# A three-block model on one core: forget attention in six half-rate stages, and four other waiting products moved

## The chip, the cores and the metric

The kernel runs on one core of a Trainium2 chip. The metric is device time in microseconds (us), the median of several runs. TensorE multiplies (PE in the profile, its weight loads PEld), VectorE (DVE) and ScalarE (ACT) do the elementwise work, GpSimd (POOL) and SyncE (SP) issue transfers here. Results of products land in PSUM, which has eight banks; everything else works in SBUF.

## What is computed

256 tokens of width 1024 go through two blocks of float32 arithmetic. The first has two layers (chunked retention, then MoBA attention), each followed by a squared-relu MLP. The second mixes four branches (a difference attention, a "forgetting" attention, a 31-tap convolution with a layer norm, a short convolution), gates them, adds a cross attention to a memory of 256 rows, and ends in a gated feed-forward. Cut to the parts that the change touches:

```python
# MoBA layer, 8 heads of 128
o = (o_own * a + o_sel * b) / (l_own * a + l_sel * b);  return o @ w_out
h = h + rms_norm(mixer(rms_norm(h, pre)), post);  h = h + rms_norm(sq_relu_mlp(rms_norm(h, mpre)), mpost)

# second block: forgetting attention, 8 heads of 64, c = cumsum(log_sigmoid(f_g + b_fgt))
s = q @ k.T * 64 ** -0.5 + (c_q - c_k);  p = softmax(where(causal, s, -inf));  yf = p @ v
yc = silu(layer_norm(dwconv_causal(...)))
# cross attention, 4 heads of 128
px = softmax(xq @ xk.T * 128 ** -0.5);  x = x + rms_norm((px @ xv) @ w_xo, norm_x_post)
```

## The kernel before, in words

**Weights.** All weights lie in 203 chunks of 128x2048 in the order of use. Each chunk is two pieces of 128x1024; SyncE loads a piece (`raw`), ScalarE copies it to a rounded high part `whi` (line 156), VectorE subtracts to the low part `wlo` (line 162). A product of float32 accuracy is then three products (`mm3`, lines 235 to 237, or `down`, lines 267 to 271): high by high, high by low, low by high.

**Units and ticks.** The program is written as a list of units of TensorE work (24 products of 256 columns, or 12 of 512). After each unit `tick()` is called: it prepares one or two more weight pieces, and lets every active "lane" do one step. A lane is a Python generator, one step up to the next `yield`; so what a lane writes in one step stands on TensorE's queue between two units, and what it needs from ScalarE and VectorE must be ready when TensorE gets there. `pipe(n, (d, f), ...)` makes a lane of `n` items: in step `j` it calls each stage `f` for item `j - d`, the deepest stage first. `slow` holds the convolution taps (line 860): one tap per tick while a lane is active, up to three otherwise. All engines work their queues in the order written; tiles come from pools with a fixed number of buffers (43 big ones of SBUF in `b4`, four PSUM banks in `psw` for short-lived results, four in `psa` for sums), and an instruction that writes a reused buffer waits for its last reader.

**Boundaries.** Between layers, `boundary` runs the last rows of a down projection for tokens 0 to 127 (`down_pass` t = 0), then the same for tokens 128 to 255 (t = 1). While t = 1 runs, VectorE and ScalarE compute the norm of the first half (`chain`); its transposes (`pt`, line 294) are put before the last item of t = 1, or behind it with `late`.

**The places that the change touches.** (1) MoBA's last heads: `moba_pv(6)` and `moba_pv(7)` (line 775) stand among the two halves of item 0 of the output projection, ahead of the boundary (lines 808 to 815). (2) `fgh`, `fgl`, the two parts of the forget gate's weights, are split at lines 910 and 911, behind the convolution's first chunks; `forget_gate` multiplies by them in `ps_ft8` (line 922). (3) The forget lane (lines 1087 to 1140) has four stages for four pairs of heads, a new pair in every step: `forget_s` (scores `sps`, masks on VectorE, exponentials on ScalarE, line 1108), `forget_n` (reciprocal, then four scalings on ScalarE, line 1118), `forget_t` (six transposes to two `ps_ft` banks, two copies on ScalarE, line 1126), `forget_y` (products `ps_fy`, line 1135, split to `brh` and `brl`). In the same steps the difference attention's last part (`ps_dyt`, line 1075) and the short convolution (`sx`, `sy`, lines 1151 to 1163) run. (4) `conv_norm` transposes its normalized values `cxn` at line 884, two yields after it has asked for them. (5) In the cross attention, `xv` (the values, 256x512) is copied from PSUM in one ScalarE instruction per token half, and `cross_o` (line 1337) writes four heads to one bank `ps_xo` and splits it at once to `xoh`, `xol`, on which the output projection `xa` waits.

Of the kernel before, what the change touches and what calls it, by code (L numbers as in the profile page):

```python
# [99 lines left out]
def tile_model(ctx: ExitStack, tc: tile.TileContext, order, wall, x, mem, gains, pparam, rparam, w_fg,  # L100
# [20 lines left out]
    def bank(name):  # L121
        return psw.tile([128, 512], F32, tag="w", name=name)
# [58 lines left out]
    def done(n=1):  # L181

        state["done"] += n
# [32 lines left out]
        while any(g in lanes or g in light or g in slow for g in gs):  # L216
            tick()

    def pipe(n, *stages, wait=0):

        for _ in range(wait):
            yield
        for j in range(n + max(d for d, _ in stages)):
            for d, f in reversed(stages):
                if 0 <= j - d < n:
                    f(j - d)
            yield


# [167 lines left out]
    def down_pass(acc, items, t, first, splits, before_last=None):  # L397
        n = len(items)
        for i in range(n):
            if callable(items[i]):  # L400
                items[i] = items[i]()
            w, ah, al = items[i]
            if i == n - 1 and before_last:
                before_last()
            down(acc, w, ah, al, t, first and i == 0, i == n - 1)
            if i < n - 1:
                if t:
                    done()
                tick(splits[i])

    def boundary(acc, items, first, gpost, gpre, fill0, fill1, mid=None, late=False, splits=((2, 2, 1), (1, 1, 0))):

        gp, gn = gain(gpost), gain(gpre)
        load_sqrt()
        before = state["nraw"], state["nprep"]
        state["nraw"], state["nprep"] = AHEAD

        def x0():
            new_x()
            to_T(xn0, 0, xh2, xl2)

        down_pass(acc, items, 0, first, splits[0])
        xn0 = chain(acc[0], gp, gn, 0, "0", between=mid)
        down_pass(acc, items, 1, first, splits[1], None if late else x0)
        if late:
            x0()
        xn1 = chain(acc[1], gp, gn, 1, "1")  # L430
        done()
        state["nraw"], state["nprep"] = before
        for i, f in enumerate(fill0):
            if i == len(fill0) - 1:
                to_T(xn1, 1, xh2, xl2)
            f()
        for f in fill1:
            f()
# [330 lines left out]
    def moba_pv(hd):  # L769
        i, k = hd // 4, hd % 4  # L770
        if k == 0:
            mo[i] = b4([128, 4, 256], f"moh{i}", F32R), b4([128, 4, 256], f"mol{i}", F32R)
        po = bank("ps_mo")
        for j in range(2):
            nc.tensor.matmul(po[:, 0:256], mv[i][:, j, k * 128:k * 128 + 128],
                             mpT[hd // 2][:, hd % 2, j * 256:j * 256 + 256], start=j == 0, stop=j == 1)
        split(mo[i][0][:, k, :], mo[i][1][:, k, :], po[:, 0:256])
# [28 lines left out]
    moba_pv(4)  # L806
    moba_pv(5)
    it = moba_item(0)
    for t in range(2):
        down(acc, *it, t, True, False)  # L810
        moba_pv(6 + t)
    done()
    items = [moba_item(c) for c in range(1, 4)]
    acts, fill = mlp_start(1)
    boundary(acc, items, False, "ln_mix_post_1", "ln_mlp_pre_1", *fill)
    if upto == 3:
        return finish()
    state["nprep"] = NPREP[3]
# [8 lines left out]
    def nat_spec(name, w, c0):  # L827
        def evac(t, ps):
            if t == 0:
# [2 lines left out]

        return [("cols512", w, c0 // 512, c) for c in range(2)], evac

    boundary(acc, items, False, "ln_mlp_post_1", "norm_mix_pre_2",
             *as_group([nat_spec("av", "w_in_2", A_V), nat_spec("fv", "w_in_2", F_V)]))
    if upto == 4:
# [7 lines left out]
    def br(i):  # L845
        brh[i] = b4([128, 4, 256], f"brh{i}", F32R)
        brl[i] = b4([128, 4, 256], f"brl{i}", F32R)
# [16 lines left out]
    def conv_norm():  # L864
        ba, pts = stat("ba", 4), []
        for t in range(2):
            pts.append(bank("ps_ct"))
            for i in range(4):
                nc.tensor.transpose(pts[t][:, i * 128:i * 128 + 128], yc[:, i, tok(t)], ident)
        yield  # L870
        for t in range(2):
            bs = stat("bs", 6)
            nc.vector.bn_stats(bs, pts[t])
            nc.vector.bn_aggr(ba[:, 2 * t:2 * t + 2], bs)
        r = rstd(ba[:, 1:4:2], 2, 1.0, "ln")
        xns = [t2("cxn") for _ in range(2)]
        for t in range(2):
            nc.vector.tensor_scalar(xns[t], pts[t], ba[:, 2 * t:2 * t + 1], r[:, t:t + 1], op0=ALU.subtract, op1=ALU.mult)
        yield
        yield  # L880
        br(2)
        pts = [bank("ps_ct2") for _ in range(2)]
        for t in range(2):
            transposes(pts[t], xns[t])
        for t in range(2):
            for i in range(4):
                nc.scalar.activation(xns[t][:, tok(i)], pts[t][:, tok(i)], AF.Silu, bias=ppc("ln_b", i), scale=ppc("ln_g", i))
        for t in range(2):
            split(brh[2][:, :, tok(t)], brl[2][:, :, tok(t)], tiles(xns[t]))
        yield  # L890
# [16 lines left out]

    lf = cp.tile([128, 2, 8], F32, name="lf")

    fgh, fgl = [t1(f"fg{i}", (128, 8, 8), F32R) for i in range(2)]  # L910
    split(fgh, fgl, fg)

    cum = t1("cum", (128, 256), F32R)
    head = cp.tile([128, 8], F32R, name="head")
    lf4 = t1("lf4", (128, 2, 128))

    def forget_gate():
        ft = bank("ps_ft8")  # L920
# [36 lines left out]
        nc.vector.scalar_tensor_tensor(ls[:, 2:3], ls[:, 0:1], -1.0, ls[:, 1:2], op0=ALU.mult, op1=ALU.add)  # L957
        nc.vector.tensor_scalar(ls[:, 3:4], ls[:, 2:3], -lambda_init, None, op0=ALU.add)
        nc.vector.tensor_scalar(dn, rp[:, RP_DN:RP_DN + 128], 1.0 - lambda_init, None, op0=ALU.mult)
        nc.vector.memset(lf4, 0.0)  # L960
        nc.vector.tensor_copy(lf4.rearrange("p t (g c) -> p t g c", c=32)[:, :, :, 0:8],
                              lf[:, :, None, :].broadcast_to([128, 2, 4, 8]))
# [6 lines left out]
        pc = bank("ps_cum")  # L969
        nc.tensor.matmul(pc[:, 0:256], lf4[:, 0, :], small[:, C_TRI:C_TRI + 256], start=True, stop=False)  # L970
        nc.tensor.matmul(pc[:, 128:256], lf4[:, 1, :], small[:, C_TRI:C_TRI + 128], start=False, stop=True)
        nc.scalar.activation(cum, pc[:, 0:256], AF.Copy)
        for r in (slice(32, 64), slice(96, 128)):
            nc.vector.tensor_tensor(cum[r, :], pc[r, 0:256], cum[r, :].bitcast(F32), op=ALU.subtract)
# [112 lines left out]
    def forget_s(hp):  # L1087

        st = stat("fst", 16)
        e = b4([128, 2, 384], "fe")  # L1090
        half = [slice(0, 64), slice(64, 128)]
        for t in range(2):
            nk = 128 * (t + 1)
            for c in range(2):
                pick = head[half[c], 2 * hp + c:2 * hp + c + 1].broadcast_to([64, 128])
                nc.tensor.matmul(sps[c][:, KS[t]], pick, cum[half[c], 0:nk], start=True, stop=False)
            for c in range(2):
                nc.tensor.matmul(sps[c][:, KS[t]], fqT[half[c], hp, tok(t)], fkT[half[c], hp, 0:nk], start=False, stop=True)
        for t in range(2):
            msk = small[:, C_MASK + 128 * (1 - t):C_MASK + 256]  # L1100
            for c in range(2):
                nc.vector.tensor_tensor_reduce(e[:, c, KS[t]], sps[c][:, KS[t]], msk, scale=1.0, scalar=NEG,
                                               op0=ALU.add, op1=ALU.max, accum_out=st[:, 2 * t + c:2 * t + c + 1])
        nc.vector.tensor_scalar(st[:, 4:8], st[:, 0:4], -0.125, None, op0=ALU.mult)
        for t in range(2):
            for c in range(2):
                l = 2 * t + c
                nc.scalar.activation(e[:, c, KS[t]], e[:, c, KS[t]], AF.Exp, bias=st[:, 4 + l:5 + l], scale=0.125,
                                     accum_out=st[:, 8 + l:9 + l])
        fp[hp] = e, st  # L1110

    def forget_n(hp):
        e, st = fp[hp]
# [3 lines left out]
                l = 2 * t + c  # L1117
                nc.scalar.activation(e[:, c, KS[t]], e[:, c, KS[t]], AF.Copy, scale=st[:, 12 + l:13 + l])  # L1118

    def forget_t(hp):  # L1120
        e, _ = fp.pop(hp)
        pT = fpT[hp] = b4([128, 2, 384], "fpT")
        for c in range(2):
            pt = bank("ps_ft")
            transposes(pt, e[:, c, :], 3)
            nc.scalar.activation(pT[:, c, :], pt[:, 0:384], AF.Copy)  # L1126

    def forget_y(hp):
        py = bank("ps_fy")
# [7 lines left out]
            br(1)  # L1137
        split(brh[1][:, hp, :], brl[1][:, hp, :], py[:, 0:256])

    fl = lane(pipe(4, (0, forget_s), (1, forget_n), (2, forget_t), (3, forget_y)))  # L1140


    sbt = None
# [182 lines left out]
    for c in range(2):  # L1326
        ws_chunk(("colsat", "w_xq_2", c * 256),
                 lambda ps: nc.scalar.activation(xq[:, 2 * c:2 * c + 2, :], tiles(ps, 256), AF.Copy))
        if c == 0:
            lane(xlane)  # L1330
    as_pair(*nat_spec("xv", "w_xkv_2", 512), mth, mtl)
    drain(xlane)
    xv = nat["xv"]
    oh = b4([128, 4, 256], "xoh", F32R)
    ol = b4([128, 4, 256], "xol", F32R)

    def cross_o(t):
        po = bank("ps_xo")
        for hd in range(4):
            for j in range(2):  # L1340
                nc.tensor.matmul(po[:, hd * 128:hd * 128 + 128], xv[:, j, hd * 128:hd * 128 + 128],
                                 xpT[hd // 2][:, hd % 2, j * 256 + t * 128:j * 256 + t * 128 + 128],
                                 start=j == 0, stop=j == 1)
        split(oh[:, :, tok(t)], ol[:, :, tok(t)], tiles(po))

    cross_o(0)
    acc = [pair("xa0"), pair("xa1")]
# [241 lines left out]
```

## Time and profile before

| | |
|---|---|
| median of 3 runs | 1264.92 us (1264.87 to 1265.36) |
| the profiled execution | 1264.71 us |
| its span in the trace | 1263.0 us |
| granted clock of TensorE over the span | 0.999 |
| busy: PE, PEld, DVE, ACT | 1237.4, 1115.1, 877.7, 678.4 us |
| transfers | 227.43 MB, 180 GB/s |

How to read it: an engine's row in a timeline gives start, duration, source line, the tile written and those read, and in brackets how long the engine had been idle and what ended that. TensorE's products overlap: one of 256 columns is shown with 0.28 us, one of 512 with 0.39, while the next starts after 0.12 or 0.23. So a wait is best read from start to start.

### The profile page before, as it was taken

What the parts mean: (1) busy time and instruction counts of PE and PEld (TensorE: products, weight loads), DVE (VectorE), ACT (ScalarE), POOL (GpSimd) and SP (SyncE); (2) the same over time, 40 slices, a digit from 0 to 9 for tenths busy, and PEclk for the clock granted to TensorE, in tenths of its full rate; (3) what the DMA queues carried; (4) which work ended last, traced back from release to release, by engine and by line L of the source; (5) the groups of instructions that cost most, each with busy time, mean ns of one, the idle gap of its engine ahead of it and who ended that gap; (6) DMA issues with size and microseconds to landing.
All of it is one profiled execution on the core that took longest, in us unless ns stands there. A gap on an engine that the chain in (4) does not pass through costs nothing. (4 is left out here: it accounts for less than half of the span.)

```text
span 1263.0 us, 20014 instructions
## 1 busy us (share of the span) xinstructions
PE 1237.4 (98%) x7870; PEld 1115.1 (88%) x7870; DVE 877.7 (69%) x1537; ACT 678.4 (54%) x1103; POOL 9.3 (1%) x22
## 2 busy tenths in 40 slices
PE   6999999999999999999999999999999999999997
PEld 4888888899988888899998999899999897899996
DVE  6774768755566766765557578688877877588773
ACT  5553445644444765654444545754446575666552
POOL 0000000000000000000000000000000000000000
PEclk9999999999999999999999999999999999999999
DMA  9765564665664535566565644255665564455530
GB/s 342 279 186 156 159 218 166 213 196 178 198 217 134 183 120 180 187 214 190 179 211 181 208 144 141 71 174 170 188 203 197 182 207 163 159 191 185 183 117 34
DMA packets 64206, 227.43 MB, mean 180 GB/s; under 512 B 8048, under 2 KB 8304, under 8 KB 64112
## 3 DMA queue, kind: packets, MB, share of 16 engines
q1 hardware_dynamic: 61808, 217.76, 52.8%
q0 software_dynamic: 2304, 8.39, 2.0%
q8 instruction: 62, 1.02, 0.3%
q14 instruction: 32, 0.26, 0.1%
HBM read 225.08 MB, written 1.05 MB: 179 GB/s over the span
## 5 line engine op out<-in xcount | busy, mean ns | idle before, releaser
L162 DVE TENSOR_TENSOR wlo<-raw,whi 128x1024 fp32r<-128x1024 f32 x406 | 480.1, 1220 | 79.9 <-ACT whi L156 78.8
L156 ACT ACTIVATE whi<-raw 128x1024 fp32r<-128x1024 f32 x406 | 406.8, 1049 | 52.8 <-PE ps_ws L237 14.8
L235 PE MATMUL ps_ws<-xhi,whi 128*128 128x256 f32 x1376 | 391.3, 284 | 1.2 <-ACT fpT L1126 0.9
L236 PE MATMUL ps_ws<-xlo,whi 128*128 128x256 f32 x1376 | 389.3, 283 | 0.0
L237 PE MATMUL ps_ws<-xhi,wlo 128*128 128x256 f32 x1376 | 389.3, 283 | 0.0
L235 PEld LDWEIGHTS ps_ws<-xhi,whi 128*128 128x128 f32 x1376 | 263.8, 192 | 5.9 <-issue 2.5
L236 PEld LDWEIGHTS ps_ws<-xlo,whi 128*128 128x128 f32 x1376 | 263.9, 192 | 1.5
L237 PEld LDWEIGHTS ps_ws<-xhi,wlo 128*128 128x128 f32 x1376 | 263.9, 192 | 0.0
L235 PE MATMUL ps_as<-whi,xhi 128*128 128x512 f32 x352 | 142.2, 404 | 0.3 <-ACT xhi L231 0.3
L236 PE MATMUL ps_as<-wlo,xhi 128*128 128x512 f32 x352 | 137.7, 391 | 0.5 <-DVE wlo L162 0.5
L237 PE MATMUL ps_as<-whi,xlo 128*128 128x512 f32 x352 | 138.1, 392 | 0.0
L268 PE MATMUL mlp<-wlo,act 128*128 128x512 f32 x240 | 93.7, 390 | 0.0
L267 PE MATMUL mlp<-whi,act 128*128 128x512 f32 x240 | 93.5, 390 | 0.0
L237 PEld LDWEIGHTS ps_as<-whi,xlo 128*128 128x128 f32 x352 | 66.2, 188 | 15.3 <-DVE xlo L232 1.1
L236 PEld LDWEIGHTS ps_as<-wlo,xhi 128*128 128x128 f32 x352 | 66.5, 189 | 14.2 <-DVE wlo L162 1.3
L235 PEld LDWEIGHTS ps_as<-whi,xhi 128*128 128x128 f32 x352 | 66.4, 189 | 13.6 <-ACT xhi L231 0.9
L662 DVE SCALAR_TENSOR_TENSOR relu<-ps_ws,relu 128x512 f32<-128x512 f32 x24 | 16.6, 691 | 87.1 <-ACT relu L661 87.1
L661 ACT ACTIVATE relu<-ps_ws 128x512 f32<-128x512 f32 x24 | 14.4, 598 | 113.8 <-PE ps_ws L237 113.8
L271 PE MATMUL mlp<-whi,act 128*128 128x512 f32 x240 | 73.9, 389 | 0.0
L271 PEld LDWEIGHTS mlp<-whi,act 128*128 128x128 f32 x240 | 45.1, 188 | 9.5
L267 PEld LDWEIGHTS mlp<-whi,act 128*128 128x128 f32 x240 | 45.2, 188 | 8.6
L268 PEld LDWEIGHTS mlp<-wlo,act 128*128 128x128 f32 x240 | 45.2, 188 | 8.6
(427 smaller groups left out, 1613.8 us busy)
## 6 DMA issues: line engine op xcount, KB each, us to landing
raw<-in_wall_dram SPq DMA_DIRECT2D x406, 512.0 KB, 4.2
h<-in_x_dram SPq DMA_DIRECT2D x4, 256.0 KB, 5.7
gainln_mix_post<-in_gains_dram POOLq DMA_DIRECT2D x2, 512.0 KB, 5.6
gainln_mlp_pre<-in_gains_dram POOLq DMA_DIRECT2D x2, 512.0 KB, 6.7
gainln_mlp_post<-in_gains_dram POOLq DMA_DIRECT2D x2, 512.0 KB, 7.6
mem<-in_mem_dram POOLq DMA_DIRECT2D x2, 512.0 KB, 5.8
out_dram<-h SPq DMA_DIRECT2D x4, 256.0 KB, 2.9
dec<-in_t_dec_dram SPq DMA_DIRECT2D x2, 384.0 KB, 8.9
```

The lines of the kernel that those rows point to most:

```text
L156: nc.scalar.activation(hi, raw, AF.Copy)
L162: nc.vector.tensor_tensor(lo, raw, hi.bitcast(F32), op=ALU.subtract)
L235: nc.tensor.matmul(o, ah, bh, start=start, stop=False)
L236: nc.tensor.matmul(o, ah, bl, start=False, stop=False)
L237: nc.tensor.matmul(o, al, bh, start=False, stop=stop)
L267: nc.tensor.matmul(acc[t][n], ah[:, k, ts], wh[k][:, ns], start=st, stop=False)
L268: nc.tensor.matmul(acc[t][n], ah[:, k, ts], wl[k][:, ns], start=False, stop=False)
L271: nc.tensor.matmul(acc[t][n], al[:, k, ts], wh[k][:, ns], start=False, stop=False)
L661: nc.scalar.activation(r, ps, AF.Relu)
L662: nc.vector.scalar_tensor_tensor(r, ps, 0.0, r, op0=ALU.max, op1=ALU.mult)
```

## The change

It has five parts. MoBA: both halves of heads 6 and 7 come before the boundary, item 0's second token half moves into the boundary's t = 1 pass as its first item (`ahead`). Forget gate: `fgh`, `fgl` are split before the preceding boundary; `lf4` and `cum` are taken from their pool later. Forget lane: the exponentials become a stage of their own, the transposes of a pair are put in two steps, and a new pair starts in every second step; the lane has 12 steps in place of 7. Convolution norm: one more yield ahead of the transposes of `cxn`. Cross attention: `xv` of the second token half is copied in two halves, and `cross_o` writes two heads to each of two banks, each split by itself.

```diff
-    def pipe(n, *stages, wait=0):
+    def pipe(n, *stages, wait=0, every=1):
-        for j in range(n + max(d for d, _ in stages)):
+        for j in range(every * (n - 1) + 1 + max(d for d, _ in stages)):
             for d, f in reversed(stages):
-                if 0 <= j - d < n:
-                    f(j - d)
+                if 0 <= j - d < n * every and (j - d) % every == 0:
+                    f((j - d) // every)
...
-        down_pass(acc, items, 1, first, splits[1], None if late else x0)
+        down_pass(acc, [*ahead, *items], 1, first or bool(ahead), splits[1], None if late else x0)
...
-    for t in range(2):
-        down(acc, *it, t, True, False)
-        moba_pv(6 + t)
-    done()
+    down(acc, *it, 0, True, False)
+    for hd in (6, 7):
+        moba_pv(hd)
...
-    boundary(acc, items, False, "ln_mix_post_1", "ln_mlp_pre_1", *fill)
+    boundary(acc, items, False, "ln_mix_post_1", "ln_mlp_pre_1", *fill, ahead=[it])
...
+    fgh, fgl = [t1(f"fg{i}", (128, 8, 8), F32R) for i in range(2)]
+    split(fgh, fgl, fg)
     boundary(acc, items, False, "ln_mlp_post_1", "norm_mix_pre_2",
...
         yield
         yield
+        yield
         br(2)
...
-        for t in range(2):
-            for c in range(2):
-                l = 2 * t + c
-                nc.scalar.activation(e[:, c, KS[t]], e[:, c, KS[t]], AF.Exp, ...)
+    def forget_e(hp):
+        e, st = fp[hp]
+        ...
+    def forget_t(hp, c):
+        if c == 0:
+            fpT[hp] = b4([128, 2, 384], "fpT")
+        pt = bank("ps_ft")
+        transposes(pt, fp[hp][0][:, c, :], 3)
+        nc.scalar.activation(fpT[hp][:, c, :], pt[:, 0:384], AF.Copy)
...
-    fl = lane(pipe(4, (0, forget_s), (1, forget_n), (2, forget_t), (3, forget_y)))
+    fl = lane(pipe(4, (0, forget_s), (1, forget_e), (2, forget_n), (3, lambda hp: forget_t(hp, 0)),
+                   (4, lambda hp: forget_t(hp, 1)), (5, forget_y), every=2))
...
+            for sl in (slice(0, 256), slice(256, 512)):
+                nc.scalar.activation(xv[:, t, sl], ps[:, sl], AF.Copy)
...
-        po = bank("ps_xo")
-        for hd in range(4):
+        for i in range(2):
+            po = bank("ps_xo")
+            for k in range(2):
+                hd = 2 * i + k
...
-        split(oh[:, :, tok(t)], ol[:, :, tok(t)], tiles(po))
+            split(oh[:, 2 * i:2 * i + 2, tok(t)], ol[:, 2 * i:2 * i + 2, tok(t)], tiles(po[:, 0:256]))
```

ScalarE's queue in the forget lane, one step of the program before (`fe` are the probabilities, L1118 scales those of one pair, L1108 takes the exponentials of the next, `whi` begins each step):

```order
L156 ACTIVATE whi<-raw 128x1024
L231 ACTIVATE brh_7913<-ps_fy 128x256
L1126 ACTIVATE fpT<-ps_ft 128x384 x2
L1118 ACTIVATE fe<-fe,fst 128x128 x2
L1118 ACTIVATE fe<-fe,fst 128x256 x2
L1108 ACTIVATE fe,fst<-fe,fst 128x128 x2
L1108 ACTIVATE fe,fst<-fe,fst 128x256 x2
L1151 ACTIVATE sx<-ps_ws 128x256
L156 ACTIVATE whi<-raw 128x1024
```

The same place in the changed program, the sixth and seventh step (L1114 now takes the exponentials, L1123 scales, L1130 copies the transposes):

```order
L156 ACTIVATE whi<-raw 128x1024
L231 ACTIVATE brh_7991<-ps_fy 128x256
L1130 ACTIVATE fpT<-ps_ft 128x384
L1114 ACTIVATE fe,fst<-fe,fst 128x128 x2
L1114 ACTIVATE fe,fst<-fe,fst 128x256 x2
L1156 ACTIVATE sx<-ps_ws 128x256
L231 ACTIVATE brh_7661<-ps_dyt 128x4x128
L156 ACTIVATE whi<-raw 128x1024
L1130 ACTIVATE fpT<-ps_ft 128x384
L1123 ACTIVATE fe<-fe,fst 128x128 x2
L1123 ACTIVATE fe<-fe,fst 128x256 x2
```

A step now has either the exponentials of one pair or the scalings of another, and one copy of transposes, where each step had both and two copies.

TensorE's queue at the end of MoBA before: item 0 for t = 0 ends, head 6 follows, then item 0 for t = 1 (`moba_0_4564`).

```order
L271 MATMUL moba_1_4563<-whi,mol_4459 128x512
L775 MATMUL ps_mo<-mpT,mv_4480 128x256 x2
L267 MATMUL moba_0_4564<-whi,moh_4458 128x512
L268 MATMUL moba_0_4564<-wlo,moh_4458 128x512
L267 MATMUL moba_1_4565<-whi,moh_4458 128x512
```

The same place in the changed program:

```order
L271 MATMUL moba_1_4563<-whi,mol_4459 128x512
L777 MATMUL ps_mo<-mpT,mv_4480 128x256 x4
L267 MATMUL moba_0_4562<-whi,moh_4458 128x512
L268 MATMUL moba_0_4562<-wlo,moh_4458 128x512
L267 MATMUL moba_1_4563<-whi,moh_4458 128x512
```

Both heads' products stand together, and t = 0 goes on; the twelve products of item 0 for t = 1 follow behind the whole pass t = 0.

ScalarE's queue at the cross attention before (`xv` values, `xoh` the heads' results):

```order
L831 ACTIVATE xv<-ps_as 128x512
L156 ACTIVATE whi<-raw 128x1024
L231 ACTIVATE xoh<-ps_xo 128x4x128
L395 ACT_TABLE_LOAD
```

and in the changed program:

```order
L1343 ACTIVATE xv<-ps_as 128x256 x2
L156 ACTIVATE whi<-raw 128x1024
L231 ACTIVATE xoh<-ps_xo 128x2x128 x2
L395 ACT_TABLE_LOAD
```

Each of the two copies is now two of half the width; the weight copy stays between them.

## Rows read from the trace of the kernel before

**Rows 1.** The page's first part: busy us, share of span, instructions.
```profile
span 1263.0 us, 20014 instructions
PE 1237.4 (98%) x7870; PEld 1115.1 (88%) x7870; DVE 877.7 (69%) x1537; ACT 678.4 (54%) x1103; POOL 9.3 (1%) x22
```

**Rows 2.** PE's longest wait, whole run: us in total, times, longest.
```profile
PE pt L294 <- DVE xn L391: 10.9, 1, 10.9
```

**Rows 3.** Timeline of PE at MoBA's boundary: start, us, instruction [idle before].
```profile
500.06 0.39 PE L268 MATMUL moba<-wlo,moh 128*128 128x512 f32 x1
500.28 0.61 PE L271 MATMUL moba<-whi,mol 128*128 128x512 f32 x2
501.48 1.09 PE L294 MATMUL pt<-ident,y 128*128 128x128 f32 x8 [0.59 <-DVE y L391]
```

**Rows 4.** Timeline of PE at the forget gate's product.
```profile
736.04 0.28 PE L236 MATMUL ps_ft<-xlo,fg 128*8 128x256 f32 x1
737.28 0.28 PE L237 MATMUL ps_ft<-xhi,fg 128*8 128x256 f32 x1 [0.96 <-DVE fg L232]
737.40 0.28 PE L235 MATMUL ps_ft<-xhi,fg 128*8 128x256 f32 x1
```

**Rows 5.** Timeline of PE in the forget lane, steps 3 to 6 of 7.
```profile
804.04 0.84 PE L294 MATMUL ps_ft<-ident,fe 128*128 128x128 f32 x5 [0.36 <-ACT fe L1118]
...
809.76 0.87 PE L294 MATMUL ps_ft<-ident,fe 128*128 128x128 f32 x6
810.56 0.33 PE L1096 MATMUL sps<-cum,head 64*128 64x128 f32 x2
...
812.61 0.39 PE L235 MATMUL ps_ws<-xhi,whi 128*128 128x256 f32 x1 [0.90 <-ACT fpT L1126]
...
816.48 0.92 PE L294 MATMUL ps_ft<-ident,fe 128*128 128x128 f32 x6
817.99 0.66 PE L294 MATMUL ps_dyt<-ident,dsq 128*128 128x128 f32 x4 [0.58 <-ACT fpT L1126]
...
822.24 0.55 PE L294 MATMUL ps_ft<-ident,fe 128*128 128x128 f32 x3
...
824.18 0.66 PE L294 MATMUL ps_dyt<-ident,dsq 128*128 128x128 f32 x4 [0.32 <-ACT fpT L1126]
825.15 0.39 PE L235 MATMUL ps_ws<-xhi,whi 128*128 128x256 f32 x1 [0.32 <-DVE brl L232]
```

**Rows 6.** Step 4 in the table by windows: length, then busy PE, PEld, DVE, ACT, POOL.
```profile
808.90:815.60 6.70, 5.80 (x52) 4.80 (x50) 3.46 (x14) 6.70 (x24) 0.00 (x0) 1.00 0.28 81
```

**Rows 7.** ACT's groups by line in the forget lane: busy, mean ns | idle before.
```profile
L1118 ACT ACTIVATE fe<-fe,fst 128x128 f32<-128x128 f32 (+1 forms) x16 | 6.0, 445 | 2.9 <-DVE fst L1114 2.9
L231 ACT ACTIVATE brh<-ps_fy 128x256 fp32r<-128x256 f32 x4 | 1.5, 369 | 2.7 <-PE ps_fy L1135 2.7
```

**Rows 8.** Timeline of PE at the convolution norm's transposes.
```profile
954.45 1.28 PE L294 MATMUL ps_ct<-ident,cxn 128*128 128x128 f32 x8 [0.48 <-DVE cxn L878]
```

**Rows 9.** Timeline of ACT at the cross attention.
```profile
1049.31 0.60 ACT L831 ACTIVATE xv<-ps_as 128x512 f32<-128x512 f32 x1 [2.09 <-PE ps_as L237]
1049.80 1.05 ACT L156 ACTIVATE whi<-raw 128x1024 fp32r<-128x1024 f32 x1
1051.88 0.60 ACT L231 ACTIVATE xoh<-ps_xo 128x512 fp32r<-128x512 f32 x1 [1.03 <-PE ps_xo L1341]
```

**Rows 10.** Timeline of PE at the cross attention.
```profile
1049.96 1.83 PE L1341 MATMUL ps_xo<-xpT,xv 128*128 128x128 f32 x14 [0.47 <-ACT xv L831]
1052.53 0.50 PE L267 MATMUL xa<-whi,xoh 128*128 128x512 f32 x1 [0.75 <-ACT xoh L231]
...
1060.76 0.50 PE L267 MATMUL xa<-whi,xoh 128*128 128x512 f32 x1 [0.69 <-ACT xoh L231]
```

**Rows 11.** Timeline of DVE there: the first token half's norm, last step.
```profile
1065.46 0.89 DVE L391 TENSOR_SCALAR y<-y,s 128x512 f32<-128x512 f32 x2
```

**Rows 12.** The page's list of transfers: weight pieces, KB each, us to landing.
```profile
raw<-in_wall_dram SPq DMA_DIRECT2D x406, 512.0 KB, 4.2
```

More of the change, by code (lines that the diff above doesn't have):

```diff
@@ L409, in down_pass, with boundary @@
                 tick(splits[i])
-    def boundary(acc, items, first, gpost, gpre, fill0, fill1, mid=None, late=False, splits=((2, 2, 1), (1, 1, 0))):
+    def boundary(acc, items, first, gpost, gpre, fill0, fill1, mid=None, late=False, splits=((2, 2, 1), (1, 1, 0)),
+                 ahead=()):
         gp, gn = gain(gpost), gain(gpre)
@@ L908, in tile_model @@
     lf = cp.tile([128, 2, 8], F32, name="lf")
-    fgh, fgl = [t1(f"fg{i}", (128, 8, 8), F32R) for i in range(2)]
-    split(fgh, fgl, fg)
-    cum = t1("cum", (128, 256), F32R)
+    fsum = {}
     head = cp.tile([128, 8], F32R, name="head")
-    lf4 = t1("lf4", (128, 2, 128))
     def forget_gate():
@@ L959, in forget_gate @@
         nc.vector.tensor_scalar(dn, rp[:, RP_DN:RP_DN + 128], 1.0 - lambda_init, None, op0=ALU.mult)
+        lf4 = t1("lf4", (128, 2, 128))
         nc.vector.memset(lf4, 0.0)
@@ L971, in forget_gate @@
         nc.tensor.matmul(pc[:, 128:256], lf4[:, 1, :], small[:, C_TRI:C_TRI + 128], start=False, stop=True)
+        cum = fsum["cum"] = t1("cum", (128, 256), F32R)
         nc.scalar.activation(cum, pc[:, 0:256], AF.Copy)
@@ L1095, in forget_s @@
                 pick = head[half[c], 2 * hp + c:2 * hp + c + 1].broadcast_to([64, 128])
-                nc.tensor.matmul(sps[c][:, KS[t]], pick, cum[half[c], 0:nk], start=True, stop=False)
+                nc.tensor.matmul(sps[c][:, KS[t]], pick, fsum["cum"][half[c], 0:nk], start=True, stop=False)
             for c in range(2):
@@ L1104, in forget_s @@
         nc.vector.tensor_scalar(st[:, 4:8], st[:, 0:4], -0.125, None, op0=ALU.mult)
+        fp[hp] = e, st
+    def forget_e(hp):
+        e, st = fp[hp]
         for t in range(2):
@@ L1109, in forget_s @@
                                      accum_out=st[:, 8 + l:9 + l])
-        fp[hp] = e, st
     def forget_n(hp):
@@ L1118, in forget_n @@
                 nc.scalar.activation(e[:, c, KS[t]], e[:, c, KS[t]], AF.Copy, scale=st[:, 12 + l:13 + l])
-    def forget_t(hp):
-        e, _ = fp.pop(hp)
-        pT = fpT[hp] = b4([128, 2, 384], "fpT")
-        for c in range(2):
-            pt = bank("ps_ft")
-            transposes(pt, e[:, c, :], 3)
-            nc.scalar.activation(pT[:, c, :], pt[:, 0:384], AF.Copy)
+    def forget_t(hp, c):
[4 more added lines that the diff above has]
+        nc.scalar.activation(fpT[hp][:, c, :], pt[:, 0:384], AF.Copy)
     def forget_y(hp):
@@ L1330, in tile_model, with xv_evac @@
             lane(xlane)
-    as_pair(*nat_spec("xv", "w_xkv_2", 512), mth, mtl)
+    xv = b4([128, 2, 512], "xv")
+    def xv_evac(t, ps):
+        if t == 0:
+            nc.scalar.activation(xv[:, t, :], ps, AF.Copy)
+        else:
+            for sl in (slice(0, 256), slice(256, 512)):
+                nc.scalar.activation(xv[:, t, sl], ps[:, sl], AF.Copy)
+    as_pair([("cols512", "w_xkv_2", 1, c) for c in range(2)], xv_evac, mth, mtl)
     drain(xlane)
-    xv = nat["xv"]
     oh = b4([128, 4, 256], "xoh", F32R)
@@ L1337, in cross_o @@
     def cross_o(t):
-        po = bank("ps_xo")
-        for hd in range(4):
[L1340 to L1343, printed above, removed]
-        split(oh[:, :, tok(t)], ol[:, :, tok(t)], tiles(po))
+        for i in range(2):
+            po = bank("ps_xo")
+            for k in range(2):
+                hd = 2 * i + k
+                for j in range(2):
+                    nc.tensor.matmul(po[:, tok(k)], xv[:, j, tok(hd)],
+                                     xpT[i][:, k, j * 256 + t * 128:j * 256 + t * 128 + 128], start=j == 0, stop=j == 1)
+            split(oh[:, 2 * i:2 * i + 2, tok(t)], ol[:, 2 * i:2 * i + 2, tok(t)], tiles(po[:, 0:256]))
     cross_o(0)
```

## The prediction

> **What bounds the kernel now.** I read the page's first part first: TensorE is busy 1237.4 of 1263.0 us, the next engine 69% [rows 1]. The end of the program is therefore set by TensorE's queue, and a change that neither adds nor removes products can only move the 25.6 us in which TensorE is idle. Next I read the waits of PE over the whole run: 10.9 us of the idle time is the start of the program, before the first normalized rows exist [rows 2], and no edit comes near it. So all that this change can reach lies in short stalls of 0.3 to 1.2 us in the middle. The view for these is the timeline of PE at each place that the diff names. There the reader is to look at starts, not at the idle time in brackets: a product's shown end is later than the moment at which the next could start, so the bracket is always some 0.15 us short of the true loss (0.96 in brackets, 1.24 against 0.12 from start to start [rows 4]).
>
> **The terms.** The products are the same in number and shape before and after; five stalls are to be priced.
>
> *MoBA's boundary.* The last two products ahead of the transposes start from 500.28 on, the usual spacing is 0.22 to 0.23 (500.06 to 500.28), and the transposes start at 501.48, held by the norm on VectorE [rows 3]: 1.20 - 2 x 0.23 = 0.74 us lost. The change puts twelve products of 0.23, 2.7 us, between the end of t = 0 and these transposes, which is work taken from ahead of the boundary. The norm starts as much earlier as TensorE's sum is ready earlier, so 2.7 us of cover stand against 0.74 of lateness: the stall goes whole, **0.74**. Heads 6 and 7 cost what they cost before; their split is needed only by the third item behind them.
>
> *Forget gate.* The third product waits for the low part `fg` that VectorE writes behind convolution taps: 1.24 from start to start, 0.12 is usual [rows 4]. Splitting it a boundary earlier removes the wait: **1.12**. What it adds is one small instruction each on ScalarE and VectorE ahead of a norm that waits for TensorE anyway; I cost it at nothing. If that cover were gone it would be about 0.4 (two instructions, no more than the 128x256 copy's 0.37 each [rows 7], in part side by side).
>
> *Forget lane.* Waits in the seven steps now: 0.36 in step 3; 0.90 in step 4; in step 5 six transposes and then `ps_dyt` take 1.51 where six undisturbed take 0.80 (809.76 to 810.56), so 0.71; in step 6 six transposes and four `ps_dyt` take 2.91 (822.24 to 825.15) where ten take 1.3 at the pace of 0.80 for six, so 1.6 [rows 5]. Together 3.6. In step 4 ScalarE is busy for all of its 6.70 us [rows 6], and the scalings wait for the reciprocals [rows 7]: the step asks more of ScalarE than TensorE's 24 weight products of 0.12 and the lane's own products cover. Half-rate stages remove this for steps 3 to 5: a step now has four exponentials or four scalings, not both. What stays: the first transposes come one step behind their scalings, whose reciprocal stands on VectorE behind the difference attention's scaling: I take 0.2. And the two `ps_dyt` groups keep their two neighbouring steps, now with one shared PSUM bank (the pool gives the second the first one's bank; before they had two), while the short convolution, the masks and a weight piece stand on VectorE ahead of their last reader. Neither row shows this new order. Its cost is bounded below by 0 and above by a little over today's 1.6 in the step with `ps_dyt`; I take 1.6, the nearest row, since the same readers are late there today. More steps mean more places where the lane's products interrupt the weight products, but each of the eight blocks of half-width products is still entered and left once, so I cost the interruptions at 0 (at most 0.1 for each of the four transposes split in two). Net 3.6 - 1.6 - 0.2, **1.8** (0 to 3.6).
>
> *Convolution norm.* Eight transposes wait 0.48 in brackets and take 1.28 where eight take 1.09 at another place [rows 8, 3], as the second half of their input is late as well: 0.67, with the bracket's shortfall about **0.75**. One more unit of weight products (2.9 us) now stands ahead. What follows, silu and split on ScalarE, ends a step later; the branch products that read it stand several units further on.
>
> *Cross attention.* Token half 0: the second product waits for the whole `xv` copy, which takes 0.60 from 1049.31 [rows 9]; a copy of half the width takes 0.37 [rows 7], so TensorE goes on 0.23 earlier. Then `xa` starts at 1052.53 because `xoh` is made after all sixteen records of `ps_xo` [rows 10]. With two banks the first half of `xoh` needs eight of them. It then hangs on ScalarE: from 1049.31 two copies of 0.37, the weight copy 1.05, and 0.37 for `xoh` give 1051.5, and TensorE's sixteen records end at about 1051.4. Gain 1052.53 - 1051.5 = **1.05**. Token half 1: 0.69 in brackets [rows 10], some 0.85 from start to start, and here ScalarE is free; but then the first half's norm is late next: its last step ends at 1066.35 [rows 11], just as TensorE now starts the transposes. VectorE's split in that chain becomes shorter (its first half lies beside TensorE's second), so I give back 0.1: **0.75**.
>
> [...] The row shows 0.37 for half and 0.60 for the whole [rows 7, 9], so a split costs 0.14. [...]
>
> **The sum.** 0.74 + 1.12 + 1.8 + 0.75 + 1.05 + 0.75 = 6.2 us. The profiled execution took 1264.71, so 1258.5; the median of the three runs is 0.2 above that execution, so I forecast **1258.7**. About 0.2%, 2.5 us, is what a measurement of this kernel can tell from no change: the line is at 1262.4.
>
> **Rivals.**
>
> *A. PSUM banks hold the forget lane, not the pace.* Two of today's waits there are for a bank's reader (`fpT`, `brl` [rows 5]), and the lane now needs a bank in nearly every step, eleven of twelve. For it: the shared bank of `ps_dyt`. Against it: six transposes took two banks in one step, now three take one. If each saved wait returns as a bank wait, the lane gains 0 and the time is 1260.5. The Trainium skill ("Perfetto Trace Analysis", Optimization Strategy) reads gaps that repeat on the saturated engine as a sign that too few PSUM or SBUF buffers are there; the waits for `fpT` in steps 4 to 6 agree with that, the reciprocal wait of the scalings does not. Chance 0.2.
>
> *B. All stalls go.* If the readers of `ps_dyt` keep up once ScalarE has air, 1.8 more are saved, and the brackets' shortfalls another 0.4: 1256.5. Against it: VectorE's queue there is as long as before in the same two steps. Chance 0.15.
>
> *C. Little is left.* Stalls close one after the other on one queue; if TensorE, once earlier, meets the next late input at each place (weight pieces, the norm in [rows 11], silu), only the MoBA and the gate terms stay, 1.86 less 0.4: 1263.2. Against it: no weight piece is waited for at these places in the rows. Chance 0.08.
>
> *D. Slower.* Item 0's four weight buffers are now held until the boundary's second pass, some 11 us longer, and the forget lane's `fe` tiles some twice as long; both share the pool in which pieces land, and loads are issued in order on one queue. A piece takes 4.2 us from issue to landing [rows 12]. If the pieces due behind such a hold come late, TensorE stands for about one landing each: with three of them, 12.6 us, 1271. It decides once the hold exceeds the lead, and eight or nine pieces are prepared ahead at these places in the written order, one of which is used in each unit of 2.9 us. Chance 0.04, and 0.03 of it is over the line.
>
> **How the numbers follow.** The forecast's case has 0.53 (1257.5 to 1259.9, as the lane's residual lies between 0.5 and 2.9), A 0.2, B 0.15, C 0.08, D 0.04. The range takes in B's and A's times with the scatter of their terms, and leaves out C and D and the edges of B, under 0.2: 1256.2 to 1261.4. Faster by over 0.2%: the forecast, A and B, 0.88; within 0.2%: C and a part of D, 0.09; slower: 0.03.
>
> **What would show it.** In the changed profile: no wait of the MoBA transposes for `y`; none of `ps_ft` for `fg`; no wait for `fe` or `fpT` in step 4's place, and the largest wait of the lane at the second `ps_dyt` or the unit behind it; none at `ps_ct`; `xa` starting at the first token half within 0.3 us of the last `ps_xo` record. PE busy stays at about 1237 and the span falls. The prediction is wrong if the lane's waits stay near 3.6 in sum (A), if they vanish (B), or if PE shows new waits for `wlo` or `whi` behind MoBA's boundary or in the forget lane (D).

## The result and the profile after

The changed kernel takes **1258.34 us** (median of 4 runs, 1258.06 to 1259.14) against 1264.89 for the kernel before in the same comparison: a ratio of 0.995, 95% interval 0.9937 to 0.9963, faster by 6.55 us where 6.2 were forecast. Its profiled execution took 1259.14 us with a span of 1257.0.

The page's first part and the waits of PE over the whole run (total in us, times, longest) answer to [rows 1, 2]:

```profile
span 1257.0 us, 20022 instructions
PE 1236.1 (98%) x7870; PEld 1115.4 (89%) x7870; DVE 877.4 (70%) x1539; ACT 678.3 (54%) x1106; POOL 9.3 (1%) x22
```

```profile
PE pt L294 <- DVE xn L391: 11.2, 1, 11.2
PE ps_dyt L294 <- DVE brl L232: 1.1, 1, 1.1
PE pt L294 <- DVE mtl L232: 0.7, 1, 0.7
PE ps_xo L1356 <- ACT xv L1343: 0.3, 1, 0.3
PE ps_as L235 <- ACT xhi L231: 0.3, 1, 0.3
PE ps_ws L235 <- ACT fpT L1130: 0.2, 1, 0.2
```

The waits for `y` at MoBA's boundary, `fg`, `fe` and `xoh` are no longer among the largest. Two large ones are left behind the program's start: the second `ps_dyt`, which was foreseen, and transposes waiting for `mtl`, the low part of the cross attention's memory, which were not. The timeline of PE shows each place; the transposes at MoBA's boundary now follow the products at their usual distance, 0.46 behind the start of the last two [rows 3]:

```profile
500.39 0.39 PE L268 MATMUL moba<-wlo,moh 128*128 128x512 f32 x1
500.61 0.62 PE L271 MATMUL moba<-whi,mol 128*128 128x512 f32 x2
501.07 0.93 PE L294 MATMUL pt<-ident,y 128*128 128x128 f32 x7
...
735.57 0.28 PE L236 MATMUL ps_ft<-xlo,fg 128*8 128x256 f32 x1
735.69 0.28 PE L237 MATMUL ps_ft<-xhi,fg 128*8 128x256 f32 x1
...
804.67 0.80 PE L294 MATMUL ps_ft<-ident,fe 128*128 128x128 f32 x3
...
813.94 0.55 PE L294 MATMUL ps_ft<-ident,fe 128*128 128x128 f32 x3
815.54 0.66 PE L294 MATMUL ps_dyt<-ident,dsq 128*128 128x128 f32 x4 [1.05 <-DVE brl L232]
816.41 0.39 PE L235 MATMUL ps_ws<-xhi,whi 128*128 128x256 f32 x1 [0.22 <-ACT fpT L1130]
...
968.83 0.60 PE L294 MATMUL pt<-ident,mem 128*128 128x128 f32 x4
970.12 0.66 PE L294 MATMUL pt<-ident,mem 128*128 128x128 f32 x4 [0.70 <-DVE mtl L232]
...
1045.46 1.83 PE L1356 MATMUL ps_xo<-xpT,xv 128*128 128x128 f32 x14 [0.25 <-ACT xv L1343]
1047.05 0.47 PE L267 MATMUL xa<-whi,xoh 128*128 128x512 f32 x1
...
1054.66 0.48 PE L267 MATMUL xa<-whi,xoh 128*128 128x512 f32 x1
```

The gate's third product follows after 0.12 [rows 4], and `xa` starts at both token halves without a wait [rows 10]. Start to start, the forget lane keeps 0.25 inside its first transposes, 1.2 ahead of the second `ps_dyt` (815.54) and 0.46 ahead of the unit behind it (0.49 behind the last of the four `ps_dyt`, where 0.03 is usual): 2.0 in all, with 0.06 inside the `ps_dyt`. The memory's second transposes start 1.29 behind the first four, where four take 0.43: 0.9 with what follows.

**Place by place.** TensorE runs 7870 products in both programs, so a product of the same number, ahead of and behind a place, is the same product. The difference between its start in one trace and in the other, taken on both sides of a place, is what the place gained, with no idle time to interpret:

| place (products by number) | gained, us | forecast |
|---|---|---|
| MoBA's boundary (2500 to 2750) | 0.90 | 0.74 |
| forget gate (4000 to 4250) | 1.07 | 1.12 |
| forget lane (4500 to 5000) | 2.43 | 1.8 |
| convolution norm, then memory norm (5750 to 6000 to 6250) | 0.89, then -0.59: 0.30 | 0.75 |
| cross attention (6500 to 6750) | 1.63 | 1.8 |
| sum | 6.33 | 6.2 |

From product 250 on, the difference changes by under 0.03 between these places. It starts at -0.43: this profiled execution began 0.3 later, and the start (the wait for `xn`, 10.2 to 11.2 us over the profiles shown here) differs more from one execution to the next than the stretches between the places do. In the experiments below, "the lane" and "the place" stand for this difference against the changed kernel's trace; it tells 0.1 us, the medians about half a microsecond.

### The profile page after: what moved, and what is told of

The parts are those of the page before. It is cut to its first block, busy times and chain, and to the rows that moved or that the text cites. A ratio compares the mean times of both kernels' runs of the same rounds, so it can differ in the third digit from the quotient of the medians.

```text
span 1257.0 us, 20022 instructions
## 1 busy us (share of the span) xinstructions
PE 1236.1 (98%) x7870; PEld 1115.4 (89%) x7870; DVE 877.4 (70%) x1539; ACT 678.3 (54%) x1106; POOL 9.3 (1%) x22
## 4 chain that ended last, share of the span: by engine, by line
PE 94%; DVE 2%; ACT 2%; issue 1%; DMA 1%; SPq 0%; DVEq 0%
PE ps_ws L235 13%; PE ps_ws L237 13%; PE ps_ws L236 13%; PE ps_as L237 6%; PE ps_as L235 6%; PE ps_as L236 6%; PE mlp L268 4%; PE mlp L267 4%; PE mlp L271 4%; PE ffn L268 1%; PE ffn L271 1%; PE ffn L267 1%; PE ps_br L235 1%; PE ps_br L236 1%; PE ps_br L237 1%; PE pt L294 1%
```

## The experiments

All kernels but the last two are the changed kernel with one edit; the last two change two places each.

### The lane: rate, stages, and both

The lane of before, four stages and a new pair in every step, in the changed kernel (`lane_full4`):

```diff
+    def forget_se(hp):
+        forget_s(hp)
+        forget_e(hp)
+    def forget_tt(hp):
+        forget_t(hp, 0)
+        forget_t(hp, 1)
-    fl = lane(pipe(4, (0, forget_s), (1, forget_e), (2, forget_n), (3, ...), (4, ...), (5, forget_y), every=2))
+    fl = lane(pipe(4, (0, forget_se), (1, forget_n), (2, forget_tt), (3, forget_y)))
```

> The changed kernel with the forget lane of before: four stages, a new pair of heads in every step; all other parts of the change stay. Theory (the half rate saved 1.6 us of waits net): the lane's waits are again about 3.6 us and the time is 1.4 to 1.8 us longer, about 1259.9. Rival (the waits in the lane depend on what lies around it): under 2.5 us of waits, and the time within 0.6 us of the changed kernel.

1261.32 us (ratio to before 0.9971, interval 0.9961 to 0.9982): 3.0 longer by the medians, and the lane loses 2.43, exactly what it had gained and more than the theory's 1.4 to 1.8. The rival is out; what is left of the change gains 3.6.

Half of the lane's change, the rate alone (`lane_half4`, the same edit with `every=2`), and the other half, the stages alone (`lane_full6`, `every=2` taken out):

> The changed kernel with four stages (exponentials in the step of their scores, six transposes in one step), but a new pair in every second step. Theory (it is the rate that matters, four exponentials or four scalings for each step in place of both): the waits of the lane are 1.0 to 2.2 us, the time within 0.6 us of 1258.3. Rival (the exponentials' own stage matters): the first transposes wait again 0.5 us or more in several steps, over 2.8 us of waits, the time 0.8 to 1.6 us longer.

> The changed kernel with its six stages, but a new pair of heads in every step. Theory (the rate matters): waits of 3 to 4 us in the lane, time about 1259.8. Rival (the stages matter, not the rate): waits within 0.5 us of the changed kernel's 2.0, time within 0.5 us of 1258.3.

Neither theory nor rival holds. `lane_half4` takes 1264.91 us (ratio 1.0, 0.9991 to 1.0008) and `lane_full6` 1264.79 (0.9999, 0.999 to 1.0007): each half of the edit makes the lane slower than before, by 6.7 and 6.1 us against the changed kernel where the lane of before costs 2.43. Only together do they gain. Two more kernels part the stages at half rate, `half_exp` with the exponentials in a step of their own, `half_split` with the transposes in two steps:

```diff
+    # half_exp
+    fl = lane(pipe(4, (0, forget_s), (1, forget_e), (2, forget_n), (3, forget_tt), (4, forget_y), every=2))
+    # half_split
+    fl = lane(pipe(4, (0, forget_se), (1, forget_n), (2, lambda hp: forget_t(hp, 0)),
+                   (3, lambda hp: forget_t(hp, 1)), (4, forget_y), every=2))
```

> The changed kernel with five stages at half rate: the exponentials in a step of their own, but all six transposes of a pair in one step. Theory (at half rate the exponentials in the step of their scores make ScalarE wait for the masks, and VectorE's reciprocal then waits behind ScalarE; the stage of their own is what the half rate needs): the lane costs at most 1 us more than in the changed kernel, time 1257.8 to 1259.3. Rival (the transposes in two steps are what the half rate needs, as they take one bank of PSUM in a step in place of two): 3 us or more above the changed kernel, 1261.3 or more.

> The changed kernel with five stages at half rate: the exponentials in the step of their scores, the six transposes of a pair in two steps. Theory (the exponentials' place decides): the lane costs 4 to 7 us more than in the changed kernel, 1262.3 to 1265.3, and ScalarE stands idle over 2 us ahead of the exponentials. Rival (the split of the transposes decides): at most 1 us more, 1259.3 or less.

`half_exp` takes 1259.39 us (0.9956, 0.9944 to 0.9969), just over the theory's range, its lane 0.48 more than the changed kernel's; `half_split` 1263.15 (0.9987, 0.9978 to 0.9996), its lane 4.8 more. So the exponentials' own step is what the half rate needs; splitting the transposes adds 0.5 to it, and without it 1.9 (6.7 less 4.8). Why shows best in the first pair of `half_split`, in the timeline of PE, then of VectorE and of ScalarE:

```profile
793.76 0.39 PE L235 MATMUL ps_ws<-xhi,whi 128*128 128x256 f32 x1
...
799.48 0.28 PE L237 MATMUL ps_ws<-xhi,wlo 128*128 128x256 f32 x1
800.86 0.33 PE L294 MATMUL ps_ft<-ident,fe 128*128 128x128 f32 x1 [1.09 <-ACT fe L1123]
801.55 0.44 PE L294 MATMUL ps_ft<-ident,fe 128*128 128x128 f32 x2 [0.36 <-ACT fe L1123]
```

```profile
798.59 0.17 DVE L1066 TENSOR_TENSOR drl<-drl,z_dif 128x8 f32<-128x8 f32 x1
798.68 1.22 DVE L162 TENSOR_TENSOR wlo<-raw,whi 128x1024 fp32r<-128x1024 f32 x1
799.82 0.46 DVE L863 SCALAR_TENSOR_TENSOR yc<-cu,pp,yc 128x238 f32<-128x238 f32 x1
800.19 0.17 DVE L1119 RECIPROCAL fst<-fst 128x4 f32<-128x4 f32 x1
```

```profile
800.40 1.49 ACT L1123 ACTIVATE fe<-fe,fst 128x128 f32<-128x128 f32 x4 [0.95 <-DVE fst L1119]
```

The scores end where the weight products go on, at 793.76, and the second of the transposes gets its input at 801.55: 7.8 us. ScalarE is idle for 0.95 right ahead of the scalings, so it isn't ScalarE's load; the reciprocal stands in VectorE's queue behind the difference attention's norm, a weight piece and a tap. It does not wait for ScalarE here, as the theory of `half_exp` had it: the exponentials of this pair are done at 798.0. In the other three pairs ScalarE does wait ahead of the exponentials for the masks of the same step, 7.0 us in three waits of up to 3.0, as expected; what these cost TensorE was not taken apart.

In the kernel before, the first pair's chain takes the same time: its scores end at 796.24 and the second of its transposes starts at 804.04, 7.8 as well.

```profile
796.24 0.39 PE L235 MATMUL ps_ws<-xhi,whi 128*128 128x256 f32 x1
...
803.35 0.33 PE L294 MATMUL ps_ft<-ident,fe 128*128 128x128 f32 x1
804.04 0.33 PE L294 MATMUL ps_ft<-ident,fe 128*128 128x128 f32 x1 [0.36 <-ACT fe L1118]
```

But TensorE comes for it after 7.1 us before (803.35) and after 5.8 at half rate, because the step in between no longer holds the next pair's scores. Half rate shortens the steps, and with the same number of steps a pair has less time. With a step of their own for the exponentials, TensorE comes later by one unit and by the next pair's scores: in the changed kernel the scores end at 794.70 (the next weight product) and the first transposes start at 804.67, 10.0 us later. The chain has grown there too, as the reciprocal stands a step further down VectorE's queue:

```profile
803.68 0.17 DVE L1119 RECIPROCAL fst<-fst 128x4 f32<-128x4 f32 x1
```

The second of the transposes starts at 805.03, 10.3 us behind the scores. So at the first pair TensorE arrives ahead of that input by 0.7 us in the kernel before, by 2.0 at half rate with the old stages, and by 0.3 with the exponentials' own step. In `lane_half4` the late scalings cost 1.8 us at the first pair and 2.2 at the last (832.80); banks whose readers stand on VectorE cost 2.7 more, and the clock, shown below, 1.7. Less the changed kernel's 2.0 that is 6.4 of its 6.7.

In `lane_full6` it is another wait. Four scalings and four exponentials of one step stand on ScalarE ahead of a copy out of a bank, of `sx` at the first wait and of `ps_dyt` at the second, and the banks stay held. Ahead of the second wait's copy the scalings start at 816.69, 1.88 late for their reciprocals, and the copy itself at 820.15. The waits of PE, and that copy on ScalarE:

```profile
PE ps_ft L294 <- DVE brl L232: 3.1, 1, 3.1
PE ps_dyt L294 <- DVE sx L1157: 2.0, 1, 2.0
```

```profile
820.15 0.57 ACT L231 ACTIVATE brh<-ps_dyt 128x512 fp32r<-128x512 f32 x1
```

Both slow kernels and `half_split` pay for their waits a second time: behind a pair of waits TensorE's granted clock falls to 0.50, 1.2 GHz, for 3.4 us. The table by windows of `lane_full6` (length, busy us of PE, PEld, DVE, ACT, POOL, then the granted clock) shows it just behind the wait that ends at 821.50:

```profile
820.00:822.00 2.00, 0.50 (x3) 0.31 (x3) 1.67 (x3) 2.00 (x5) 0.00 (x0) 1.00 0.00 0
822.00:824.00 2.00, 1.69 (x8) 1.38 (x8) 1.37 (x4) 1.22 (x4) 0.00 (x0) 0.57 0.42 47
824.00:826.00 2.00, 2.00 (x12) 2.00 (x12) 0.71 (x2) 1.71 (x5) 0.00 (x0) 0.57 0.57 223
```

(1 - 0.57) x 4 is 1.7 us of full speed lost. `lane_half4` loses as much from 834.6 to 838.1, `half_split` from 802.9 to 806.3. With it most of `lane_full6` is told: its waits are 2.08, 3.19 and 0.43 beyond the usual step; less the changed kernel's 2.0 and with the 1.7 that gives 5.4 of the 6.1.

### The residual at the second ps_dyt

```diff
-            pt = bank("ps_dyt")
+            pt = psa.tile([128, 512], F32, tag="acc", name="ps_dyt")
```

The banks that the difference attention has just left take both `ps_dyt`; no instruction moves.

> The changed kernel, and the two ps_dyt results are put in the two banks of the sum pool that the difference attention's spo has just left, in place of the short-lived pool; no instruction is moved on any engine. Theory (the residual of the forget lane is the shared bank: the second ps_dyt waits until the first one's reader brl has run): the 1.30 us ahead of the second ps_dyt and the 0.26 us behind it go, the lane's waits fall from 2.0 to under 0.5, and the time to about 1256.8. Rival (pacing: ScalarE and VectorE are late in that step whatever the bank): the wait turns up one group later, the lane keeps over 1.3 us of waits, and the time stays within 0.4 us of 1258.3.

1257.33 us (0.9941, 0.9929 to 0.9954), 1.0 under the changed kernel. Its timeline of PE at the same place, and two steps on:

```profile
813.11 0.55 PE L294 MATMUL ps_ft<-ident,fe 128*128 128x128 f32 x3
813.49 0.60 PE L294 MATMUL ps_dyt<-ident,dsq 128*128 128x128 f32 x4
...
822.85 0.44 PE L294 MATMUL ps_ft<-ident,fe 128*128 128x128 f32 x2 [0.35 <-ACT fe L1123]
```

Both waits at `ps_dyt` are gone, 1.22 + 0.46 with the 0.06: no instruction moved, so the shared bank was the cause. The lane gained 1.18, not 1.7, as the transposes of the next pair now lose 0.57 from start to start, their scalings being that much too late; with the 0.25 that stayed, 0.8 us of waits are left where the theory had under 0.5. The rival's new wait is there, but the lane keeps 0.8 us of waits where it needs over 1.3.

### The convolution norm's step, and the memory norm

`conv_back` takes the additional yield out again; `mem_apart` adds one between the two token halves of the memory norm's transposes:

```diff
         yield
         yield
-        yield
         br(2)
```

```diff
             to_T(memn[t], t, mth, mtl)
             yield
+            if t == 0:
+                yield
```

> The changed kernel without the additional step ahead of the transposes of the convolution norm. Theory (that step traded one wait for another): the transposes ps_ct wait 0.75 us again, and the 0.90 us ahead of the second transposes of the memory norm go, so that the time stays within 0.4 us of 1258.3. Rival (the two waits have nothing to do with each other): both waits are there, time 0.75 us longer.

> The changed kernel with one more step between the two token halves of the memory norm's transposes. Theory (the 0.90 us at 969 is a PSUM bank's reader mtl, which stands on VectorE behind two weight pieces): the wait goes, time about 1257.4. Rival (VectorE is as far behind one step later): a wait of 0.5 us or more there or at the next unit, time within 0.4 us of 1258.3.

`conv_back` takes 1258.44 us (0.995, 0.9938 to 0.9963), the same time. Its timeline has the old wait back, and the memory's eight transposes stand in one row without one:

```profile
949.66 0.52 PE L294 MATMUL ps_ct<-ident,cxn 128*128 128x128 f32 x3 [0.48 <-DVE cxn L881]
...
968.93 1.04 PE L294 MATMUL pt<-ident,mem 128*128 128x128 f32 x8
```

It loses 0.90 at the norm and gets 0.58 back at the memory, where the unit behind the transposes starts 0.3 late again, as in the kernel before. What ties the two places is VectorE's queue, here in the changed kernel:

```profile
958.74 1.29 DVE L232 TENSOR_TENSOR brl<-cxn,brh 128x512 fp32r<-128x512 f32 x2 [4.30 <-ACT brh L231]
...
969.39 1.28 DVE L232 TENSOR_TENSOR mtl<-pt,mth 128x512 fp32r<-128x512 f32 x2
```

and in `conv_back`:

```profile
955.76 1.29 DVE L232 TENSOR_TENSOR brl<-cxn,brh 128x512 fp32r<-128x512 f32 x2 [3.25 <-ACT brh L231]
...
967.57 1.28 DVE L232 TENSOR_TENSOR mtl<-pt,mth 128x512 fp32r<-128x512 f32 x2
```

With the additional step ScalarE's silu and its copy `brh` end later, VectorE waits for them ahead of `brl`, and the memory's norm stands behind `brl` in its queue. So `mtl`, which frees the bank of the second transposes, comes 1.8 us later, while TensorE comes at the same time (968.83 and 968.93).

`mem_apart` takes 1257.93 (0.9946, 0.9932 to 0.9959). The 0.92 goes there, but 0.43 comes back at the end of the `mix` products that follow, where four products, from the first of a new sum on, start late by 0.05 to 0.16. Net 0.49, half of what the theory expected; which operand they wait for, the trace does not name.

### The cross attention

`xo_whole` has the old `cross_o`, `xv_whole` the old copy of `xv`:

> The changed kernel with one bank of four heads in the cross attention's last products, split at once, as before; the copy of xv in two halves stays. Theory (the two banks bring most of the cross attention's part): xa waits again at both token halves, 0.7 to 0.9 us at the first and 0.85 at the second, less the 0.25 that the norm's transposes lose now: 1.3 to 1.6 us longer, about 1259.8. Rival (what is won there is lost at the next late input): under 0.6 us longer.

> The changed kernel with xv of the second token half copied at once; the two banks stay. Theory (the half copy brings forward the second product of ps_xo by 0.2 us, and xa hangs on the later xoh): the wait at the second product is 0.6 in place of 0.41, and the time 0.1 to 0.3 us longer. Rival (two copies cost ScalarE more than one, and xoh stands behind them): xa starts no later than now, and the time is the same or up to 0.2 us shorter.

`xo_whole` takes 1260.01 us (0.9961, 0.9948 to 0.9973); the place loses 1.42, as expected. Both waits are those of [rows 10], to the hundredth:

```profile
1047.29 0.50 PE L267 MATMUL xa<-whi,xoh 128*128 128x512 f32 x1 [0.75 <-ACT xoh L231]
...
1055.51 0.50 PE L267 MATMUL xa<-whi,xoh 128*128 128x512 f32 x1 [0.69 <-ACT xoh L231]
```

`xv_whole` takes 1258.52 (0.9948, 0.9936 to 0.9961). Its median is 0.2 longer, which the medians cannot tell, and the place gains 0.05. Here the theory falls:

```profile
1044.90 1.83 PE L1352 MATMUL ps_xo<-xpT,xv 128*128 128x128 f32 x14 [0.47 <-ACT xv L1339]
1046.49 0.47 PE L267 MATMUL xa<-whi,xoh 128*128 128x512 f32 x1
```

The second `ps_xo` waits 0.21 longer, but `xa` loses nothing behind it, while in the changed kernel its first product by `xol` waits 0.21 and the next 0.12. What the half copy saves at one product it pays at the next one that is late. Without the two banks it does bring something: `xo_whole`, which keeps the half copy, is 1.63 - 1.42 = 0.21 ahead of the kernel before.

### MoBA and the gate

```diff
-    down(acc, *it, 0, True, False)
-    for hd in (6, 7):
-        moba_pv(hd)
+    for t in range(2):
+        down(acc, *it, t, True, False)
+        moba_pv(6 + t)
+    done()
...
-    split(fgh, fgl, fg)
     boundary(acc, items, False, "ln_mlp_post_1", "norm_mix_pre_2",
```

(with the call of the boundary as before, and the split back behind the convolution's first chunks)

> The changed kernel with MoBA's last heads, item 0 and the split of the forget gate's weights as before. Theory (both waits were whole losses): 0.74 + 1.12 us longer, about 1260.2, with the wait for y at MoBA's boundary and that for fg back in the timeline. Rival (part of the two is taken up behind, where TensorE meets an input that is late anyway): less than 1.2 us longer.

1260.53 us (0.9964, 0.9952 to 0.9977), 2.2 longer. The places lose 0.90 and 1.13, and nothing comes back behind them; the waits are those of [rows 3, 4]:

```profile
502.32 0.88 PE L294 MATMUL pt<-ident,y 128*128 128x128 f32 x6 [0.59 <-DVE y L391]
...
738.13 0.28 PE L237 MATMUL ps_ft<-xhi,fg 128*8 128x256 f32 x1 [0.96 <-DVE fg L232]
```

### A version that beats both

The two fixes above together, `ps_dyt` in banks of its own and the memory norm's transposes a step apart:

> The changed kernel with the two ps_dyt in banks of their own and one more step between the two halves of the memory norm's transposes. Theory (both residual waits are PSUM banks held by a late reader): 1.5 + 0.9 us shorter than the changed kernel, about 1255.9, and no wait over 0.5 us left on TensorE behind the start of the program. Rival (TensorE, earlier by that, meets the next late input): at least 0.8 us of it comes back, 1256.8 or more.

**1256.88 us** (0.9936, 0.9922 to 0.9949). In the trace the two places gain 1.17 and 0.46, as each did alone; the rival was right that a good part of the 2.4 comes back at the next late input. The waits of PE that are left:

```profile
PE pt L294 <- DVE xn L391: 10.2, 1, 10.2
PE ps_ft L294 <- ACT fe L1123: 0.4, 1, 0.4
PE ps_xo L1358 <- ACT xv L1345: 0.3, 1, 0.3
PE ps_as L235 <- ACT xhi L231: 0.2, 1, 0.2
```

## Why the prediction was right, and where its steps were not

The time was right, 1258.34 for 1258.7, and by its own case: PE busy stayed, the idle time fell. But the sum of 6.33 against 6.2 hides errors of up to 0.6 in both directions; that they cancel is luck.

- **MoBA's boundary** and the **forget gate**: right. `moba_fg_back` gives both back, and nothing is late next. Of the 0.90 at MoBA's boundary 0.80 is the wait; the rest comes where the products of heads 6 and 7 are put together, which the prediction had at nothing.
- **Forget lane**: 2.43 for 1.8. The residual was placed and sized nearly as predicted (1.6 foreseen at `ps_dyt` and behind, 1.7 measured; 0.2 at the first transposes, 0.25), and `dyt_own_bank` shows its cause, the bank. The waits removed were undersized: 3.6 was read where 2.43 + 2.0, or 4.4, went; 0.36 and 0.90 of it were taken from the brackets, where the starts give 0.57 and 0.97. The step that failed is the reason, "Half-rate stages remove this for steps 3 to 5: a step now has four exponentials or four scalings, not both". `lane_half4` has just that and its lane is 4.3 us slower than the one of before (6.7 - 2.43). What counts is by how much TensorE arrives ahead of the end of a pair's chain: at the first pair 0.7 us before, 2.0 by half rate alone, 0.3 with the exponentials' own step. The prediction gave that step no part in the gain; that the term came out near is luck, as rate and step are in the same edit.
- **Convolution norm**: 0.30 for 0.75. The wait went, with 0.89 even more than priced; the step that failed is that what follows, silu and split on ScalarE, "ends a step later" at no cost. The prediction followed it to the branch products; the cost lies on VectorE, which waits for that split with the memory's norm behind it, and so in the memory norm's second transposes, five units on.
- **Cross attention**: 1.63 for 1.8. The two banks bring 1.42 of it on top of the half copy, and all of it without (`xv_whole`). The half copy's 0.23 was counted in full; it brings 0.21 without the two banks and nothing beside them, as the products by `xol`, which the prediction did not price, are then late. The half copies took 0.38, near the row's 0.37. The norm's transposes, which wait 0.25, were given 0.1.
- **Rivals**: A is out (`lane_full4` loses the lane's whole gain), though its mechanism, banks, makes up all of the residual at `ps_dyt`. B's last 1.8 did not go by itself; `dyt_own_bank` gets 1.18 of it. C's picture, one late input closing behind another, is true at three small places (memory, `xol`, the norm's transposes), not at the large ones. D did not occur: no wait for `wlo` or `whi` is among the waits of PE, so weight buffers held longer cost nothing. The Trainium skill's reading of repeated gaps as possibly too few PSUM or SBUF buffers ("Perfetto Trace Analysis", Optimization Strategy) fits `ps_dyt`; it does not fit the first waits of `half_split`, 1.25 and 0.58, which are for late scalings.

## What to carry to other kernels

A software pipeline's stage needs time, not steps: when the rate is halved, the steps get shorter, and a chain that nearly fitted into two of them no longer does, so change rate and stage count together and compare the chain's length in us with the distance at which the consumer comes. Read both again after the edit: a stage more moves the chain's own instructions down their queues too. Read what an edit brings from the start of the same product ahead of and behind each place, in both traces; it tells 0.1 us where medians tell half a microsecond, and it shows what a place further on gives back. Where a group waits on a shared PSUM bank, look for a bank that another phase has just left before moving any instruction.

## What the runs showed of the hardware that was not expected

A wait of 3.2 us that followed another of 2.1 us some 7 us earlier was followed by a granted clock of 0.50 for about 3.4 us (1.7 lost at half speed) right behind it (`lane_full6`), so the wait cost 1.7 us more than its own length. In `half_split` waits of 1.25 and 0.58 close together came ahead of the same fall. The same two waits at the same place in `lane_half4` brought none; its fall came later, behind 1.62 and 0.58. So the length of the waits alone does not tell which of them is punished, and what does was not settled here. Nor need it come in every execution: the mean granted clock of `half_split` is 0.997 to 0.999 over eleven executions, and the two at 0.999 are the shortest, 1262.30 and 1262.46 against a median of 1263.15; no trace of these two was kept.
